# Other gather rates by stage in a one-core decoder layer, and half of one list's rows made by ACT

## The chip, the core and the metric

The kernel runs on one core of a Trainium2 chip. The metric is the device time of one execution in microseconds (us), as the median of several runs. The core has five instruction queues: PE (TensorE, matrix products), DVE (VectorE), ACT (ScalarE), POOL (GpSimd, which here issues all indirect DMAs) and SP (SyncE, which issues most other DMAs). Each queue runs its instructions in order and waits on semaphores of the others.

## What is computed

One decoder layer on 256 tokens of width 2048: attention, a PEER feed-forward, a gated embedding, with a layer norm behind each. The change lies in the PEER part, which the reference computes so:

```python
q = (xt @ wq).reshape(t, PEER_HEADS, PEER_QDIM)
sa = jnp.einsum('thc,nc->thn', qa, sub_keys[0]); sb = jnp.einsum('thc,nc->thn', qb, sub_keys[1])
va, ia = lax.top_k(sa, PEER_TOPK); vb, ib = lax.top_k(sb, PEER_TOPK)
cand = va[..., :, None] + vb[..., None, :]; cidx = ia[..., :, None] * PEER_NKEYS + ib[..., None, :]
top, sel = lax.top_k(cand, PEER_TOPK)
eidx = take_along_axis(cidx, sel); gates = softmax(top)
act = gelu(einsum('the d,td->the', u[eidx], x))
out = einsum('the,thed->td', gates * act, v[eidx])
```

Every token picks, in each of 8 heads, 16 of 16384 experts; an expert is one row of 2048 numbers in u and one in v.

## The kernel before

**Two ways for the experts.** The first 88 tokens go the sparse way: POOL gathers 128 rows of u at a time (one expert row for each of 128 partitions, 1 MB, tile `gb`, four buffers), DVE multiplies them with the tokens and sums (L951), later the same with rows of v (L961). That takes 88 gathers of u and 88 of v (`GROUPS`: 64 + 16 + 8). The other 168 tokens go the dense way: PE multiplies blocks of 128 experts with all 168 tokens, and gates are then set at the right places.

**The dense way has three stages.** *Direct blocks of u*: 68 blocks `ia`, straight from u (`u_block`, L1197; results in A0 and A1). *Listed blocks of u*: of the other 60 x 128 experts only those that some token picked, gathered by a list of their numbers: 40 blocks `b` (`CAPS[1]`), whose rows (`uf`, L1271) PE must first transpose (`ps_T`, L1280) before the products (L1289). *Blocks of v*: 46 and then 40 listed blocks (`CAPS`), each with a gather of v rows (`vf`) and one of weights (`wc`), L1256, both through POOL, up to LEAD = 4 blocks ahead; the products are L1341. DVE multiplies a block's `wc` with the u results in `weigh` (L1364).

**What has to happen beside it.** While PE computes the direct blocks, DVE selects the experts of the second tile of tokens (`topk_heads`), then ACT and DVE make one-hot flags of all picks which PE counts (`second_flags`: `eq` L884 or L837 and L838, `ohb` L887, counts L841), and from the counts comes the list of the second part (`list_work(flp, 1)`, the list made first), which ends in `idxV` and `idxW` (L1183, L1185). In its main loop each group of three columns needs `eqb`, two rows of `blk`, and `row`, a one-hot of the rank, all on DVE (L1165 to L1170). During the listed blocks of u the gates are built (`gate_work`: L1042, L1044 on DVE, L1048, L1049 on ACT, products `ps_G` L1056, L1057), the list of the first part is made, and the weights of the first part go out to HBM (`s_w`); during the first blocks of v the same happens to the gates of the second part. `gate_work` and the lists are Python generators, and `run(work, n)` puts n steps of them into the program after each block. `steps` says how many: 1 in the selection and the first tile's flags, 5 and 3 afterwards.

**How the gathers are paced.** `gathers(n)` after each block adds n to a sum, and each whole number in it puts one gather into the program, together with the DVE work on the gather three earlier (`run(sparse, 1)`, `use`). Up to the end of the direct blocks a gather is also preceded by a mark, a tiny DMA on SP's queue behind the weight loads, on which POOL waits (L980, L981). The rates are `GQ` in the query stage (13 times), 1.5 in direct blocks 0 to 4, then `GU`, in listed blocks `GUL`, in blocks of v `GVG` and `GV`. What is left is done at the last but three block of v (L1468); three blocks are held back for the end (`STAG`), their `weigh` comes after that, and the sums of the sparse tokens are taken between the banks of those three (`third_sums`).

Most of the instructions around the change keep their order as written (`keep`). The buffers of `uf` and `vf` are those of the weight loads (`sup`, tag `wf`, five buffers in turn).

Of the kernel before, what the change touches and what calls it, by code (L numbers as in the profile page):

```python
# [14 lines left out]
ALU = mybir.AluOpType  # L15
# [4 lines left out]
P = 128  # L20
# [36 lines left out]


GQ = 2.1
GU, GUL = 0.70, 1.35  # L60
GV, GVG = 0.55, 0.55
GSCALE = 2.0 ** 15
GB = 3

EARLY, HEARLY = 5, 2
# [95 lines left out]
def build(tc, a, out):  # L161
    nc = tc.nc
# [6 lines left out]
    def pbank(pool, name, tag="bank", bufs=4):  # L169
        return pool.tile([P, 512], F32, name=name, tag=tag, bufs=bufs)  # L170
# [385 lines left out]
    for c in range(NCH):  # L556
# [8 lines left out]
        for t in range(NT):  # L565
            nc.vector.scalar_tensor_tensor(x1[t][:, s], x1[t][:, s], ALPHA, pss[t],
                                           op0=ALU.mult, op1=ALU.add)
# [53 lines left out]
    io128 = gin.tile([P, P], F16, name="io128")  # L621
# [71 lines left out]
    keep = tc.keep_in_program_order  # L693
# [140 lines left out]
    def act_one_hot(dst, pool, neg):  # L834

        d = pool.tile([P, P], F16, name="dist", tag="dist", bufs=1)
        nc.scalar.activation(d, io128, AF.Abs, bias=neg)  # L837
        nc.scalar.activation(dst, d, AF.Relu, bias=1.0, scale=-1.0)  # L838
# [71 lines left out]
    def gathers(n):  # L910

        nonlocal due
        due += n
        while due >= 1:
            due -= 1
            run(sparse, 1)
# [183 lines left out]
    def list_work(oh, part):  # L1100

        nonlocal steps
        s0, ns = PARTS[part]
        m = m16[:, s0:s0 + ns]
        ps = pbank(pa, "ps_cols")
        keep(nc.tensor.matmul(ps[:ns, :P], m, ones16, start=True, stop=True))
        cols = oh.tile([P, P], F16, name="cols", tag="cols")
        keep(nc.vector.tensor_copy(cols[:ns], ps[:ns, :P]))
        yield
        ps = pbank(pa, "ps_used")  # L1110
        keep(nc.tensor.matmul(ps[:, ns:ns + 1], cols[:ns], ones16[:ns, :1], start=True, stop=True))
        keep(nc.tensor.matmul(ps[:, :ns], ahead, m, start=True, stop=False))
        keep(nc.tensor.matmul(ps[:, :ns], cols[:ns], ahead[:ns, :ns], start=False, stop=True))
        yield
        used = oh.tile([P, SEG1 + 1], F32, name="used", tag="used")
        keep(nc.vector.tensor_copy(used[:, :ns + 1], ps[:, :ns + 1]))
        pos = oh.tile([P, SEG1], F32, name="pos", tag="pos")[:, :ns]
        rank = oh.tile([P, SEG1], F32, name="rank", tag="rank")[:, :ns]
        u = used[:, :ns]

        keep(nc.vector.scalar_tensor_tensor(pos, lin[:, :ns], used[:, ns:ns + 1], u,
                                            op0=ALU.add, op1=ALU.subtract))
        keep(nc.vector.tensor_tensor(rank, u, pos, op=ALU.subtract))
        keep(nc.vector.tensor_tensor(rank, rank, m, op=ALU.mult))
        keep(nc.vector.tensor_tensor(pos, pos, rank, op=ALU.add))
        ov = gin.tile([P, 1], F32, name=f"ov{part}")
        keep(nc.vector.tensor_scalar(ov, used[:, ns:ns + 1], -float(CAPS[part] * P), 0.0,
                                     op0=ALU.add, op1=ALU.max))
        over.append(ov)
        if len(over) > 1:  # L1130
            keep(nc.vector.tensor_tensor(total, over[0], over[1], op=ALU.add))
        yield
        pi = oh.tile([P, SEG1], U32, name="pi", tag="pi")[:, :ns]
        pj = oh.tile([P, SEG1 + 1], U32, name="pj", tag="used")[:, :ns]
        pos16 = oh.tile([P, SEG1], F16, name="pos16", tag="pos16")[:, :ns]
        rank16 = oh.tile([P, SEG1], F16, name="rank16", tag="rank16")[:, :ns]
        keep(nc.vector.tensor_copy(pi, pos))
        keep(nc.vector.tensor_single_scalar(pj, pi, P - 1, op=ALU.bitwise_and))
        keep(nc.vector.tensor_single_scalar(pi, pi, 7, op=ALU.logical_shift_right))
        keep(nc.vector.tensor_copy(pos16, pi))  # L1140
        keep(nc.vector.tensor_copy(rank16, pj))
        if part:
            steps = 5
        yield

        ps = pbank(pa, "ps_list")
        made = []

        def products():
            ia0, n, row, blk = made.pop(0)  # L1150
            for j in range(n):
                keep(nc.tensor.matmul(
                    ps[:, :2 * SEG1].rearrange("p (i b) -> p i b", i=2)[:, :, :ns],
                    row[:, j], blk[:, :, j, :], start=ia0 + j == 0, stop=ia0 + j == ns - 1))

        for ia in range(0, ns, GB):
            n = min(GB, ns - ia)

            def cut(x):
                return x[:, ia:ia + n, None]  # L1160

            row = oh.tile([P, GB, P], F16, name="row", tag="ohb", bufs=OHB)
            blk = oh.tile([P, 2, GB, ns], F16, name="blk", tag="blk", bufs=3)
            eqb = oh.tile([P, GB, SEG1], F16, name="eqb", tag="eq", bufs=OHB)[:, :n, :ns]
            keep(nc.vector.tensor_tensor(eqb, io128[:, None, :ns].to_broadcast([P, n, ns]),  # L1165
                                         cut(pos16).to_broadcast([P, n, ns]), op=ALU.is_equal))
            keep(nc.vector.tensor_scalar(blk[:, 0, :n], eqb, lin[:, 0:1], None, op0=ALU.mult))
            keep(nc.vector.tensor_tensor(blk[:, 1, :n], eqb,
                                         cut(io128).to_broadcast([P, n, ns]), op=ALU.mult))
            keep(nc.vector.tensor_tensor(row[:, :n], io128[:, None, :].to_broadcast([P, n, P]),  # L1170
                                         cut(rank16).to_broadcast([P, n, P]), op=ALU.is_equal))
            made.append((ia, n, row, blk))
            yield
            if len(made) > 2:
                products()
        while made:
            products()
        ib = oh.tile([P, SEG1 + 1], F32, name="ib", tag="used")[:, :ns]
        iv = gin.tile([P, ns], U32, name=f"idxV{part}")
        iw = gin.tile([P, ns], U32, name=f"idxW{part}")  # L1180
        keep(nc.vector.tensor_copy(ib, ps[:, :ns]))
        pia = ps[:, SEG1:SEG1 + ns]
        keep(nc.vector.scalar_tensor_tensor(iw, ib, float(ns), pia, op0=ALU.mult, op1=ALU.add))  # L1183
        keep(nc.vector.tensor_scalar(ib, ib, float(s0 * NKEY), None, op0=ALU.add))
        keep(nc.vector.scalar_tensor_tensor(iv, pia, float(NKEY), ib, op0=ALU.mult, op1=ALU.add))  # L1185
        idxV[part] = iv
        idxW[part] = iw

    def run(work, n):

        for _ in range(n):
            if next(work, "end") == "end":
                return True
        return False
# [7 lines left out]
    def W_of(ia):  # L1202
        return A0[:, ia, :] if ia < SEG0 else A1[:, ia - SEG0, :]

    steps = 1
# [26 lines left out]
    for ia in range(SEG1):  # L1232
        if ia == EARLY:
            pools.close("earlyp")
            a1p = pools.open("a1p", "right", bufs=1)
            A1 = a1p.tile([P, SEG1 - SEG0, NDT], F32, name="A1")
        u_block(ia, W_of(ia))
        run(work, steps)
        gathers(GU if ia >= EARLY else 1.5)
    while not run(work, 1):  # L1240
        pass
    pools.close("flp", "tkl")
# [55 lines left out]
    work, listing = first_part(), first_list()  # L1298
# [15 lines left out]
    for b in range(CAPS[1]):  # L1314
        if b == CAPS[1] - 5:
            while not run(work, 1):
                pass
            while not run(listing, 1):
                pass
            pools.close("a1p", "a0p")  # L1320
            g2p = pools.open("g2p", "right", bufs=1)
            G2 = g2p.tile([P, SEG2, NDT], F32, name="G2")
            wcp = pools.open("wcp", "right", bufs=1)
        ps = pbank(pp, "ps_u")
        for c in range(4):
            turn(4 * b + c + 2)
            rows_mm(ps, turned.pop(0), c)
            if b < CAPS[1] - 5:
                run(work, 1)
        nc.scalar.activation(WL[:, b, :], ps[:, :NDT], AF.Gelu_apprx_tanh)  # L1330
        run(listing, 1)
        if b >= CAPS[1] - 4:
            fetch(wcp)
        gathers(GUL)
    pools.close("utp")
    work = gate_work(ohp, (G2,), *PARTS[1], 1, True)

# [50 lines left out]
    for b in range(CAPS[0]):  # L1388
        if b == CAPS[0] - LEAD:
            while not done:  # L1390
                done = run(work, 1)
            more = nc.values_load(total[0:1, 0:1], min_val=0, max_val=NIA * NKEY)
        v_blocks(1, wcp, half)
        gathers(GVG if b < 28 else GV)
    pools.close("ohp")
    wcq = pools.open("wcq", "left", bufs=1)
    for _ in range(LEAD + 1):
# [464 lines left out]
```

## Time and profile before

| | us |
|---|---|
| median of 3 runs | 1717.5 (1717.02 to 1719.36) |
| the profiled execution, its own time | 1715.06 |
| its span, first to last instruction | 1713.1 |
| direct blocks of u: first result to last | 537.4 to 864.5 |
| listed blocks of u: up to the first product of v's banks | to 1169.4 |
| blocks of v: held blocks begin | 1572.7 |

The times of stages are us from the span's start, read from the instructions in order of time (L1200 on ACT; L1348 and L1341 on PE). In the rows of the profile, a group shows the line, the engine, the operation, out<-in, the count, then busy us, mean ns of one, and the idle time of the engine just before with what ended it. A row in order of time begins with the start and the duration. A row of a window shows for each engine its busy us and instructions, then the clock that PE was granted (1.00 is full), the share of time that DMA was busy and GB/s.

### The profile page before, as it was taken

To read this page: it belongs to the slowest core of one execution; us is meant where nothing else is said; L and a number is where in the kernel's file an instruction comes from. 1 tells how busy PE (TensorE), PEld (TensorE's weight loads), DVE (VectorE), ACT (ScalarE), POOL (GpSimd) and SP (SyncE) were. 2 spreads that over 40 slices of the span, in tenths; PEclk is the share of its full clock that TensorE was granted. 3 is DMA by queue.
4 is the path that set the end of the run, shared out by engine and by line. 5 is a ranking of instruction groups with operands and counts; after the bars stand their busy time and mean duration, and the time that the engine had idled before them with its cause. 6 is when DMAs were issued, how large, how long until landed. Compare 5 with 4: busy or idle time off the path is not lost. (4 is left out here: it accounts for less than half of the span.)

```text
span 1713.1 us, 29137 instructions
## 1 busy us (share of the span) xinstructions
PE 1670.5 (98%) x11120; PEld 1550.0 (90%) x11120; DVE 1123.5 (66%) x2135; ACT 731.5 (43%) x1823; POOL 658.6 (38%) x615
## 2 busy tenths in 40 slices
PE   9999999999999999999959999989999999999998
PEld 7888888887889999999959999989999999999786
DVE  5565588763599679767877788837666223443676
ACT  5677468753111443347036677635553000000552
POOL 0143023203264422721174434528755666673000
PEclk9999999999999999999979999999999999999999
DMA  8645644584998999998779888899999999998571
GB/s 296 198 153 167 234 157 151 163 322 156 383 395 314 393 420 417 396 421 346 270 303 377 317 330 332 330 425 416 415 349 352 419 415 396 369 353 318 172 264 50
DMA packets 93996, 533.47 MB, mean 311 GB/s; under 512 B 12940, under 2 KB 16188, under 8 KB 41084
## 3 DMA queue, kind: packets, MB, share of 16 engines
q0 software_dynamic: 48912, 327.40, 48.6%
q1 hardware_dynamic: 43212, 201.02, 31.8%
q10 hardware_dynamic: 1728, 3.15, 0.5%
q8 instruction: 89, 1.46, 0.3%
q14 instruction: 55, 0.45, 0.1%
HBM read 515.70 MB, written 15.99 MB: 310 GB/s over the span
## 5 line engine op out<-in xcount | busy, mean ns | idle before, releaser
L1341 PE MATMUL ps_v<-wc,vf 128*128 128x168 f32 x2752 | 408.2, 308 | 1.9 <-DMA vf<-v_rows,idxV 1.6
L1341 PEld LDWEIGHTS ps_v<-wc,vf 128*128 128x128 f32 x2752 | 395.2, 191 | 3.2 <-issue 2.6
L212 PE MATMUL ps_u<-XF,wf 128*128 128x168 f32 x2016 | 303.5, 308 | 0.0
L212 PEld LDWEIGHTS ps_u<-XF,wf 128*128 128x128 f32 x2016 | 288.7, 190 | 2.0 <-issue 1.0
L122 DVE TENSOR_TENSOR wl<-wf,wh 128x1024 fp32r<-128x1024 f32 (+1 forms) x199 | 212.6, 1091 | 108.2 <-ACT wh L121 106.7
L121 ACT CAST wh<-wf 128x1024 fp32r<-128x1024 f32 (+1 forms) x199 | 172.1, 893 | 221.2 <-DMA wf<-ple_gate 109.0
L951 DVE SCALAR_TENSOR_TENSOR gb<-gb,xq 128x2048 f32<-128x2048 f32 x88 | 202.1, 2305 | 56.0 <-DMA gb<-u_rows,eig 55.9
L961 DVE SCALAR_TENSOR_TENSOR y<-gb,ew,y 128x2048 f32<-128x2048 f32 x78 | 182.9, 2345 | 77.5 <-DMA gb<-v_rows,eig 76.8
L1289 PE MATMUL ps_u<-XF,uT 128*128 128x168 f32 x1280 | 215.2, 311 | 0.1
L983 POOL DMA_INDIRECT gb<-u_rows,eig x88 | 100.6, 1143 | 231.4 <-DVE gb L951 117.7
L1289 PEld LDWEIGHTS ps_u<-XF,uT 128*128 128x128 f32 x1280 | 187.4, 192 | 0.9 <-ACT uT L1283 0.3
L200 PE MATMUL ps_qk<-X,wh 128*128 128x512 f32 x512 | 185.2, 401 | 0.0
L983 POOL DMA_INDIRECT gb<-v_rows,eig x88 | 118.5, 1347 | 126.0 <-DVE y L961 84.6
L1048 ACT ACTIVATE hi<-eq,ghf 128x68 f16<-128x68 f16 (+1 forms) x336 | 113.0, 336 | 84.6 <-DVE eq L1042 83.0
L202 PE MATMUL ps_qk<-X,wl 128*128 128x256 f32 x512 | 145.7, 285 | 0.0
L1256 POOL DMA_INDIRECT wc<-s_w,idxW x86 | 115.0, 1338 | 31.3 <-issue 25.8
L1256 POOL DMA_INDIRECT vf<-v_rows,idxV x86 | 93.0, 1081 | 87.3 <-PE ps_v L1341 38.3
L1283 ACT COPY uT<-ps_T 128x512 f32<-128x512 f32 x160 | 90.6, 581 | 73.6 <-PE ps_T L1280 67.9
L200 PEld LDWEIGHTS ps_qk<-X,wh 128*128 128x128 f32 x512 | 96.4, 188 | 21.9 <-issue 1.0
L212 PE MATMUL ps_q<-XF,wf 128*128 128x256 f32 x512 | 113.8, 379 | 0.5 <-ACT eb L581 0.5
L1049 ACT ACTIVATE lo<-eq,glf 128x68 f16<-128x68 f16 (+1 forms) x336 | 112.0, 333 | 0.0
L212 PEld LDWEIGHTS ps_q<-XF,wf 128*128 128x128 f32 x512 | 95.8, 190 | 13.1 <-ACT eb L581 0.9
(332 smaller groups left out, 2598.9 us busy)
## 6 DMA issues: line engine op xcount, KB each, us to landing
wf<-peer_u SPq DMA_DIRECT2D x63, 1024.0 KB
wf<-w_qk SPq DMA_DIRECT2D x64, 512.0 KB
wf<-w_out SPq DMA_DIRECT2D x32, 512.0 KB
wf<-peer_wq SPq DMA_DIRECT2D x16, 1024.0 KB
wf<-ple_gate SPq DMA_DIRECT2D x16, 1024.0 KB
wf<-w_v SPq DMA_DIRECT2D x16, 512.0 KB
wf<-w_sv SPq DMA_DIRECT2D x15, 512.0 KB
early<-peer_u SPq DMA_DIRECT2D x5, 1024.0 KB
```

The lines of the kernel that those rows point to most:

```text
L121: self.order(nc.scalar.copy(wh, src))
L122: self.order(nc.vector.tensor_tensor(wl, src, wh.bitcast(F32), op=ALU.subtract))
L200: nc.tensor.matmul(ps, wh[:, j * P:(j + 1) * P], xt[:, dt, :], start=dt == 0, stop=False)
L202: nc.tensor.matmul(ps[:, :T], wl[:, j * P:(j + 1) * P], xt[:, dt, :T], start=False, stop=dt == ND - 1)
L212: nc.tensor.matmul(ps[:, :T - t0], wf[:, dt * P:(dt + 1) * P], xt[:, dt, t0:], start=dt == 0, stop=dt == ND - 1)
L951: keep(nc.vector.scalar_tensor_tensor(g, g, 1.0, xq[i], op0=ALU.mult, op1=ALU.mult, accum_out=eact[i][:, j:j + 1]))
L961: keep(nc.vector.scalar_tensor_tensor(ys[i], g, ew[i][:, j:j + 1], ys[i], op0=ALU.mult, op1=ALU.add))
L983: keep(nc.gpsimd.indirect_dma_start(out=g, out_offset=None, in_=a[kind], in_offset=bass.IndirectOffsetOnAxis(ap=eig[i][:, 0, j:j + 1], axi ...
L1048: nc.scalar.mul(hi[:, j, :], eq[:, j, :], ghf[:, t])
L1256: keep(nc.gpsimd.indirect_dma_start(out=dst, out_offset=None, in_=src, in_offset=bass.IndirectOffsetOnAxis(ap=idx[:, b:b + 1], axis=0)))
L1289: nc.tensor.matmul(ps[:, :NDT], uT[:, j * P:(j + 1) * P], XF[:, d, NSP:], start=d == 0, stop=d == ND - 1)
L1341: return nc.tensor.matmul(psv[d // 3][:, d % 3 * NDT:(d % 3 + 1) * NDT], vf[:, d * P:(d + 1) * P], wc, start=False, stop=last and (d % 3 = ...
```

## The change

The rates are set anew. In direct blocks from 5 on, 0.50 as long as `steps` is 1 and 0.60 afterwards, where it was 0.70. In listed blocks of u 1.40 up to block 27 and 1.00 from there, where it was 1.35. In blocks of v 0.68, where it was 0.55. The list of the first part starts at listed block 3 in place of 0. In the list of the second part, every other group of `row` is made by ACT with `act_one_hot` (two ACT instructions for each of three columns), for which one more small DVE instruction makes the negative rank.

```diff
-GU, GUL = 0.70, 1.35
-GV, GVG = 0.55, 0.55
+GU, GUF, GUL, GULS = 0.50, 0.60, 1.40, 1.00
+GV = 0.68
...
         keep(nc.vector.tensor_copy(rank16, pj))
+        keep(nc.vector.tensor_scalar(rank, pj, -1.0, None, op0=ALU.mult))
...
-            keep(nc.vector.tensor_tensor(row[:, :n], io128[:, None, :].to_broadcast([P, n, P]),
-                                         cut(rank16).to_broadcast([P, n, P]), op=ALU.is_equal))
+            if part and ia % (2 * GB):
+                for j in range(n):
+                    act_one_hot(row[:, j, :], oh, rank[:, ia + j:ia + j + 1])
+            else:
+                keep(nc.vector.tensor_tensor(
+                    row[:, :n], io128[:, None, :].to_broadcast([P, n, P]),
+                    cut(rank16).to_broadcast([P, n, P]), op=ALU.is_equal))
...
-        gathers(GU if ia >= EARLY else 1.5)
+        gathers(1.5 if ia < EARLY else GU if steps == 1 else GUF)
...
         nc.scalar.activation(WL[:, b, :], ps[:, :NDT], AF.Gelu_apprx_tanh)
-        run(listing, 1)
+        if b > 2:
+            run(listing, 1)
...
-        gathers(GUL)
+        gathers(GUL if b < 28 else GULS)
...
         v_blocks(1, wcp, half)
-        gathers(GVG if b < 28 else GV)
+        gathers(GV)
```

`act_one_hot` (L834, unchanged) computes relu(1 - |column - rank|):

```python
nc.scalar.activation(d, io128, AF.Abs, bias=neg)
nc.scalar.activation(dst, d, AF.Relu, bias=1.0, scale=-1.0)
```

## The prediction

> **What bounds the kernel now.** I read the page first, then PE's waits, the busy time by stage, and last the instructions in order of time at each place where PE stops.
>
> ```profile
> span 1713.1 us, 29137 instructions
> PE 1670.5 (98%) x11120; PEld 1550.0 (90%) x11120; DVE 1123.5 (66%) x2135; ACT 731.5 (43%) x1823; POOL 658.6 (38%) x615
> PE   9999999999999999999959999989999999999998
> ```
>
> PE is the bound: 98% busy. Only what removes or adds idle PE time, or PE work at a lowered clock, changes the time. One slice in the middle (the 21st, 857 to 899 us) is at 5 tenths. The waits of PE name it:
>
> ```profile
> PE ps_G L1056 <- DVE ohb L1044: 14.1, 1, 14.1
> PE ps_T L1280 <- DMA uf<-u_rows,idxV: 5.0, 3, 2.5
> PE ps_cnt L841 <- DVE ohb L887: 1.7, 1, 1.7
> PE ps_v L1341 <- DMA vf<-v_rows,idxV: 1.6, 2, 1.1
> ```
>
> The 14.1 us lie where the direct blocks of u end and the listed blocks begin (all engines there, in order of time):
>
> ```profile
> 857.15 0.22 DVE L1185 SCALAR_TENSOR_TENSOR idxV<-ps_list,ib 128x60 uint32<-128x60 f32 x1
> 857.29 2.28 DVE L951 SCALAR_TENSOR_TENSOR gb<-gb,xq 128x2048 f32<-128x2048 f32 x1
> 864.46 0.31 ACT L1200 ACTIVATE A<-ps_u 128x168 f32<-128x168 f32 x1 [4.25 <-PE ps_u L212]
> 877.63 0.36 DVE L1042 TENSOR_TENSOR eq<-io,iaT 128x204 f16<-128x204 f16 x1
> 877.90 0.96 POOL L983 DMA_INDIRECT gb<-u_rows,eig  x1 [0.16 <-DVE gb L951]
> 878.54 0.24 PE L1056 MATMUL ps_G<-hi,ohb 128*128 128x68 f16 x1 [14.12 <-DVE ohb L1044]
> 879.16 0.94 POOL L1271 DMA_INDIRECT uf<-u_rows,idxV  x1 [0.30 <-PE ps_G L1056]
> ```
>
> The list (idxV) is complete at 857.3, the last direct block at 864.5. Yet from 857.3 to 877.6 DVE works off sparse dot products that are ahead of the first gate work in its queue, and POOL issues their gathers ahead of the first listed rows (uf), which start only at 879.2. Both queues are a backlog of token gathers:
>
> ```profile
> mark<-c_iota SPq DMA_DIRECT2D x78, 0.0 KB
> L983 POOL DMA_INDIRECT gb<-u_rows,eig x73 | 82.7, 1132 | 227.6 <-DVE gb L951 117.0 <-DVE TV L669 49.9 <-DVE eqb L1165 28.6
> ```
>
> One mark goes with each gather until the direct blocks end, so the program puts 78 gathers there (13 x 2.1 + 5 x 1.5 + 63 x 0.70 = 78.9); the second row, POOL's groups from 0 to 864.6 us, shows that 73 had been issued by then. What the stop costs, and the later stages:
>
> ```profile
> core 0: us, PE busy (x) PEld busy (x) DVE busy (x) ACT busy (x) POOL busy (x), PEclk, DMA share, GB/s
> 810.00:858.00 48.00, 48.00 (x366) 46.58 (x366) 39.46 (x109) 2.97 (x11) 5.51 (x10) 1.00 0.69 262
> 864.50:896.00 31.50, 13.88 (x85) 11.33 (x85) 26.02 (x47) 13.35 (x48) 27.29 (x19) 0.62 0.94 358
> 896.00:1100.00 204.00, 203.58 (x1778) 200.27 (x1777) 164.96 (x348) 142.53 (x444) 85.95 (x65) 1.00 0.86 334
> 1100.00:1170.00 70.00, 64.96 (x473) 63.40 (x473) 36.11 (x21) 24.40 (x49) 32.17 (x24) 0.98 1.01 420
> 1320.00:1440.00 120.00, 118.38 (x831) 117.92 (x830) 36.24 (x28) 0.59 (x1) 80.53 (x69) 1.00 1.02 414
> 1440.00:1560.00 120.00, 120.00 (x843) 119.42 (x841) 48.35 (x55) 3.84 (x7) 81.20 (x65) 1.00 0.97 366
> L1289 PE MATMUL ps_u<-XF,uT 128*128 128x168 f32 x25 | 5.4, 363 | 0.0
> L1280 PE MATMUL ps_T<-ident,uf 128*128 128x128 f32 x24 | 4.6, 349 | 0.0
> 1102.34 0.60 PE L1280 MATMUL ps_T<-ident,uf 128*128 128x128 f32 x4
> 1102.77 1.31 PE L1289 MATMUL ps_u<-XF,uT 128*128 128x168 f32 x8
> 1103.92 0.60 PE L1280 MATMUL ps_T<-ident,uf 128*128 128x128 f32 x4
> ```
>
> From 864.5 to 896 PE got through 24 transposes, 25 matmuls of ps_u (the two group rows, of that window) and 36 small ones. At the steady pace of the last three rows, four transposes take 0.43 us and eight matmuls 1.15, so this is 6 x 0.43 + 3.1 x 1.15, with 1.3 estimated for the small ones: 7.5 of 31.5 us. The stop costs 24.0 us, 17.6 of the window idle and the rest at a mean clock of 0.62.
>
> **The change, part by part.**
>
> **Fewer gathers beside the direct blocks.** In the code, the selection has 34 steps, the first tile's flags 6 more, the transposes 2: blocks 5 to 41 run with steps = 1 and take 0.50, the 26 after them 0.60. That is 34.8 + 18.5 + 15.6 = 68.9 gathers for 78.9, so 68 marks. As 73 were issued in time, the backlog at the boundary is gone; the 68th gather goes out with block 66. Before the flags, DVE has 50 dot products in its queue for 57 (53 and 60 gathers by block 41, the products three behind), and there it mostly waits for data. The next rows are a transfer of the page's last part, DVE's largest group from 715 to 750, ACT's conversion of the indices and DVE's first flag.
>
> ```profile
> uf<-u_rows,idxV POOLq DMA_INDIRECT x40, 10.4
> L951 DVE SCALAR_TENSOR_TENSOR gb<-gb,xq 128x2048 f32<-128x2048 f32 x8 | 18.3, 2297 | 17.5 <-DMA gb<-u_rows,eig 17.5
> 727.88 0.26 ACT L817 CAST ibT<-ps_gT 128x128 f16<-128x128 f32 x1
> 749.79 0.55 DVE L884 TENSOR_TENSOR eq<-io,iaT 128x384 f16<-128x384 f16 x1
> ```
>
> The flags need ibT (728.1) and begin at 749.8, behind those eight products (17.5 us of the 35 waiting for gathers); they can begin up to 21.7 us sooner, and the list with them. The uf buffers come free as PE ends blocks 63 to 67, at 4.56 us a block (4.25 + 0.31 in ACT's row above) from 846 on, so a list ready by then is early enough: the first listed rows land before the 864.5 at which PE needs them. I take 22 of the 24.0 us as gained. If the list came no earlier at all, uf would be issued at 857.5, land 10.4 us later and keep PE waiting for 3.4: a gain of some 20. Twice that loss with its slow clock makes the lower bound, 14; the upper is 24. What is late next is PE itself. PE's 1.7 us wait for a flag, and ACT's smaller ones beside it, shrink: -1.5 (0 to -2.5).
>
> **ACT makes rows of the list of the second part.** Of 20 groups, 10 lose one DVE comparison and gain 3 rows of two ACT instructions:
>
> ```profile
> L1170 DVE TENSOR_TENSOR row<-io,rank 128x384 f16<-128x384 f16 x20 | 11.0, 550 | 0.0
> L837 ACT ACTIVATE dist<-io,niaT 128x128 f16<-128x128 f16 x59 | 23.6, 401 | 1.8
> L838 ACT ACTIVATE eq<-dist 128x128 f16<-128x128 f16 x60 | 18.5, 309 | 3.1 <-PE ps_cnt L841 1.4
> ```
>
> DVE saves 10 x 0.55 = 5.5 us; ACT gains 30 x 0.71 = 21.3, in a stage where it is busy 2.97 of 48. The new rank instruction, a small one, falls once in each list: hidden on DVE, under 0.3 us if the list were late. I count nothing: the 22 us hold it.
>
> **The first part's list three blocks later.** It ends at block 30 in place of 27; its first reader is the fetch at block 36. Nothing, behind the blocks between; without that cover, a late fetch would stop PE at the start of v.
>
> **The listed blocks of u.** 28 x 1.40 + 12 x 1.00 = 51.2 for 54. Up to block 27 that is 0.05 x 2.3 = 0.1 us of DVE a block, hidden, as PE stood only 0.4 of 204 us there. In the last 12 blocks (the 1100 to 1170 row) the weights of the first part go out and DMA is saturated at 420 GB/s; PE waits 5.0 us for uf. There 4.8 gathers of 1.049 MB (128 rows of 8 KB) go: 12 us of DMA. Some of it is lag from before: -3.5 (0 to -6.4, the waits and the 0.98 clock).
>
> **The blocks of v.** 83 x 0.68 = 56.4 for 45.7. With the others that makes 176.5 for the 2 x 88 there are. At the pace of the last window (843 matmuls in 120 us, 32 a block: 4.56 us) 0.13 more a block is 30 GB/s: 366 becomes 396, and saturation is 414. Behind the 5.16 MB of the second part's weights (128 x 60 x 168 x 4 B), at about 1316, 414 - 366 = 48 GB/s were left to catch up, 108 us, which is the saturated window; now 18 are, which lasts to the end of v. When the vf waits (1.6 us) occurred, 40 us in, the arrears would be 1.2 MB larger: 2.9 us. I take +4, from 0 to the 28 that 11 moved gathers cost if none finds a gap (11 x 1.049 MB / 414 GB/s).
>
> **The last gather.** The 176th falls in the last block of the loop, behind the fetch of block 39:
>
> ```profile
> 1560.36 2.35 DVE L961 SCALAR_TENSOR_TENSOR gb<-gb,ew 128x2048 f32<-128x2048 f32 x1 [5.87 <-DMA gb<-v_rows,eig]
> 1563.57 0.93 POOL L1256 DMA_INDIRECT vf<-v_rows,idxV  x1 [2.37 <-PE ps_v L1341]
> 1566.46 0.33 DVE L1364 TENSOR_TENSOR wc<-wc,WL 128x168 f32<-128x168 f32 x1 [2.23 <-DMA wc<-s_w,idxW]
> 1572.71 5.37 PE L1341 MATMUL ps_v<-wc,vf 128*128 128x168 f32 x36 [0.30 <-PEq L1473]
> gb<-v_rows,eig POOLq DMA_INDIRECT x88, 9.9
> ```
>
> Before, the last product ended at 1562.7. Now its gather goes out at 1564.8 at the earliest and lands 9.9 later, 1574.7. Behind its product (2.35) in DVE's queue stand the weighings of the held blocks 38 and 39 (0.6), and PE's held matmuls wait for those: 1577.6 instead of 1572.7. With a dented clock I take +6 (0 to 8). The Trainium skill, "TensorE: Matmul & The Clock Gate", section on the HAM clock gate, has the clock halve after about 3.4 us of idling and recover after as much work: by it this stop alone would cost 4.9 + 1.7; the 0.62 above bears the halving out.
>
> **Sum**: -22 - 1.5 - 3.5 + 4 + 6 = -17.0. The profiled execution took 1715.06 us (span 1713.1 and 2.0 around it): 1698.1. The median, 1717.5, lies 2.4 above it: 1700.5.
>
> **Rivals.** *The costs in v do not show*: the last gather lands in time and DMA finds gaps, while the gains reach their bounds: -24 - 2.5 - 6.4 = -32.9, 1684.6. For it: PE waited only 1.6 us in 120 saturated ones. Against: the arithmetic of the last gather. *The boundary only half heals*: another DVE item, gate work or a late list, keeps PE from starting; the gain is 12 and no wait for flags goes: -12 - 3.5 + 4 + 6 = -5.5, 1712. For it: every engine's order is fixed beforehand, so one late item holds all behind it. *v gives it back, slower than before*: DMA carries no more than its mean there, the moved gathers cost the full 28: -22 - 1.5 - 3.5 + 28 + 6 = +7, 1724.5. It decides from 21 us of added waits in v on, that is, if at least 8 of 11 gathers find no gap. Against: 366 GB/s in the last 120 us beside 414 before them. The skill's "DMA: Bandwidth & Descriptors", Specifications, gives about 358 GB/s of HBM to a core, by which v would be bound like this; 414 for 120 us contradicts it. *Nothing happens*: the boundary waits for something else that the backlog hid, 1717.
>
> **How the numbers follow.** Forecast 0.60 (1690 to 1709 from its unknowns), no costs 0.13, half healed 0.15, given back 0.07, nothing 0.05. Range 1688 to 1713: it leaves out the given back case, nothing, and most of the no-cost one. About 0.2%, 3.4 us, is what a measurement here can tell. Slower by that much: given back and a little of the tail of nothing, 0.08; within it 0.05; faster 0.87.
>
> **What would show it.** 68 marks; idxV complete before about 846; uf issued as its buffer comes free, no wait of more than 2 us of ps_G or ps_T at the boundary, no clock below 1 there; the ps_T waits at the end of the listed blocks under 2 us; DMA near 414 GB/s through the second half of v with a few us of vf waits; DVE's last product about 5 us after PE could have begun the held blocks. The prediction is wrong if the boundary still stops PE for 10 us, or if the vf waits in v exceed 15.

## The result and the profile after

| | us | against the kernel before |
|---|---|---|
| before, median of 4 runs | 1717.26 (1716.89 to 1719.36) | |
| after, median of 4 runs | 1704.05 (1700.8 to 1705.25) | ratio 0.9918 [0.99, 0.9935] |
| after, the profiled execution | 1705.25 (span 1703.4) | 9.8 below 1715.06 |
| predicted, for the median | 1700.5 (1688 to 1713) | |

The kernel is faster by 13.2 us in the median, where 17.0 were forecast, so it ends 3.5 us above the forecast time. The span, which the stages below divide, is 9.7 shorter. From here on *U* is the direct blocks (to PE's last product of them), *UL* the listed blocks of u (to the last row of `WL`, the u results of a listed block), *V* the blocks of v up to the three held ones, *end* the rest; U ends with the end of that product, the other boundaries are starts in the rows of ACT and PE.

| | U ends | UL | V | end | span |
|---|---|---|---|---|---|
| before | 864.4 | 305.2 | 403.1 | 140.4 | 1713.1 |
| after | 864.4 | 280.6 | 404.1 | 154.4 | 1703.4 |
| difference | -0.1 | -24.6 | +0.9 | +14.0 | -9.7 |

On the page, PE's slices and the clock have lost the 5 in the middle; a lower slice stands near the end, where the clock is no longer full.

```profile
span 1703.4 us, 29145 instructions
...
PE 1667.9 (98%) x11120; PEld 1549.9 (91%) x11120; DVE 1120.4 (66%) x2127; ACT 754.0 (44%) x1883; POOL 678.5 (40%) x605
...
PE   9999999999999999999999999999999999997998
...
PEclk9999999999999999999999999999999999998999
```

PE's waits name the exchange: 14.1 us for `ohb` are gone, 10.5 us for a weighing (`wc`) have come.

```profile
PE ps_v L1348 <- DVE wc L1371: 10.5, 1, 10.5
PE ps_T L1286 <- DMA uf<-u_rows,idxV: 6.5, 4, 3.2
PE ps_v L1348 <- DMA vf<-v_rows,idxV: 2.7, 3, 1.2
...
PE ps_u L212 <- DMA wf<-peer_u: 1.2, 1, 1.2
```

**The boundary from U to UL**, in order of time, with the first flag, the list, the last gather, the first listed rows and what PE does:

```profile
725.93 0.56 DVE L884 TENSOR_TENSOR eq<-io,iaT 128x384 f16<-128x384 f16 x1 [2.65 <-ACT iaT L817]
...
835.42 0.22 DVE L1191 SCALAR_TENSOR_TENSOR idxV<-ps_list,ib 128x60 uint32<-128x60 f32 x1
...
854.79 3.03 POOL L983 DMA_INDIRECT gb<-u_rows,eig  x1 [4.07 <-DVE ew L942]
...
858.13 1.19 POOL L1277 DMA_INDIRECT uf<-u_rows,idxV  x1 [0.30 <-issue]
...
864.19 0.19 PE L1056 MATMUL ps_G<-hi,ohb 128*128 128x68 f16 x1
...
867.46 1.53 PE L1286 MATMUL ps_T<-ident,uf 128*128 128x128 f32 x12 [2.15 <-DMA uf<-u_rows,idxV]
```

The flags begin 23.9 us sooner (749.79 before), the list is done 21.7 us sooner (857.15 before). PE goes on at once with gate work and waits only 2.15 us for the first rows. Those are issued at 858.1, not at 846: the last sparse gather, which itself waited for DVE, is ahead of them in POOL's queue.

**The end.** The last gather is issued 1541.56; PE reaches the held blocks at 1549.0 and stands:

```profile
1541.56 0.94 POOL L983 DMA_INDIRECT gb<-v_rows,eig  x1 [0.30 <-issue]
...
1544.17 18.82 SPq L111 DMA_DIRECT2D wf<-ple_gate  x3
...
1557.40 2.35 DVE L961 SCALAR_TENSOR_TENSOR gb<-gb,ew 128x2048 f32<-128x2048 f32 x1 [7.44 <-DMA gb<-v_rows,eig]
1559.67 0.57 DVE L1371 TENSOR_TENSOR wc<-wc,WL 128x168 f32<-128x168 f32 x2
```

```profile
1549.00 0.52 PE L1348 MATMUL ps_v<-wc,vf 128*128 128x168 f32 x2 [0.30 <-PEq L1480]
1560.05 7.93 PE L1348 MATMUL ps_v<-wc,vf 128*128 128x168 f32 x34 [10.52 <-DVE wc L1371]
```

The gather takes 15.8 us to land; its product and two weighings follow, and PE's wait of 10.5 us ends with the first weighing. The 34 products that then remain take 7.93 us, where 36 took 5.37 before: the clock is low. The windows show the stages:

```profile
core 0: us, PE busy (x) PEld busy (x) DVE busy (x) ACT busy (x) POOL busy (x), PEclk, DMA share, GB/s
864.50:896.00 31.50, 29.30 (x250) 28.91 (x247) 16.93 (x37) 19.51 (x58) 14.32 (x12) 1.00 1.01 422
...
1300.00:1420.00 120.00, 117.30 (x822) 116.61 (x822) 40.12 (x28) 1.18 (x2) 88.84 (x69) 1.00 1.02 417
1420.00:1540.00 120.00, 120.00 (x842) 119.42 (x841) 56.22 (x61) 3.25 (x6) 95.58 (x72) 1.00 1.01 412
1540.00:1600.00 60.00, 47.56 (x276) 43.81 (x275) 26.50 (x49) 12.27 (x28) 4.70 (x8) 0.80 0.57 199
```

At the boundary PE is busy 29.30 of 31.5 us for 13.88. DMA now stays at 412 GB/s to the end of V, where it had eased to 366.

### The profile page after: what moved, and what is told of

Read it like the earlier page. It is cut to its first block, busy times and chain, and to the rows that moved or that the text cites. A ratio compares the mean times of both kernels' runs of the same rounds, so it can differ in the third digit from the quotient of the medians.

```text
span 1703.4 us, 29145 instructions
## 1 busy us (share of the span) xinstructions
PE 1667.9 (98%) x11120; PEld 1549.9 (91%) x11120; DVE 1120.4 (66%) x2127; ACT 754.0 (44%) x1883; POOL 678.5 (40%) x605
## 4 chain that ended last, share of the span: by engine, by line
PE 67%; DMA 13%; DVE 10%; issue 5%; POOL 4%; ACT 1%; POOLq 0%; SPq 0%; ACTq 0%; DVEq 0%
PE ps_v L1348 16%; PE ps_u L1295 9%; PE ps_qk L200 7%; PE ps_u L212 6%; DVE gb L951 4%; PE ps_qk L202 4%; PE ps_T L1286 4%; DMA uf<-u_rows,idxV 3%; PE ps_q L212 3%; DMA gb<-u_rows,eig 3%; DMA vf<-v_rows,idxV 3%; DMA gb<-v_rows,eig 2%; PE ps_v L219 2%; PE ps_v L220 2%; PE ps_v L221 2%
## 5 line engine op out<-in xcount | busy, mean ns | idle before, releaser
L1348 PE MATMUL ps_v<-wc,vf 128*128 128x168 f32 x2752 | 414.3, 310 | 13.5 <-DVE wc L1371 10.5
L983 POOL DMA_INDIRECT gb<-u_rows,eig x88 | 113.8, 1294 | 217.2 <-DVE gb L951 111.7
L983 POOL DMA_INDIRECT gb<-v_rows,eig x88 | 129.6, 1473 | 110.2 <-DVE y L961 44.6
L1262 POOL DMA_INDIRECT vf<-v_rows,idxV x86 | 107.0, 1244 | 63.1 <-PE ps_G L1057 30.5
L1262 POOL DMA_INDIRECT wc<-s_w,idxW x86 | 105.7, 1229 | 26.6 <-issue 24.4
```

The costliest lines, as they stand in the source:

```text
L983: keep(nc.gpsimd.indirect_dma_start(out=g, out_offset=None, in_=a[kind], in_offset=bass.IndirectOffsetOnAxis(ap=eig[i][:, 0, j:j + 1], axi ...
L1262: keep(nc.gpsimd.indirect_dma_start(out=dst, out_offset=None, in_=src, in_offset=bass.IndirectOffsetOnAxis(ap=idx[:, b:b + 1], axis=0)))
L1348: return nc.tensor.matmul(psv[d // 3][:, d % 3 * NDT:(d % 3 + 1) * NDT], vf[:, d * P:(d + 1) * P], wc, start=False, stop=last and (d % 3 = ...
```

## The experiments

The theory: three things make up the result. The rates beside the direct blocks heal the boundary; the ACT rows do nothing; and the last gather, put into the program within the last block of V, lands late and takes some 14 us back. The rivals are named in the expectations. Each ratio is to the kernel before, the stages as above (all from profiled executions, which lie up to 5 us from the median of their kernel).

| | median us | ratio [95%] | U ends | UL | V | end |
|---|---|---|---|---|---|---|
| e1_v_front | 1697.17 | 0.9884 [0.9858, 0.991] | 864.5 | 280.0 | 409.2 | 141.4 |
| e2_old_u_rates | 1720.45 | 1.002 [1.0006, 1.0033] | 864.2 | 301.8 | 411.0 | 140.4 |
| e3_dve_rows | 1705.93 | 0.9935 [0.992, 0.995] | 867.3 | 279.9 | 403.7 | 154.0 |
| e4_before_late_end | 1725.93 | 1.0047 [1.0029, 1.0064] | 863.9 | 304.0 | 409.1 | 148.1 |
| e5_weigh_first | 1704.48 | 0.9921 [0.9903, 0.9939] | 862.6 | 283.4 | 404.5 | 153.4 |
| e6_mix | 1693.12 | 0.9858 [0.9841, 0.9875] | 866.9 | 279.2 | 403.4 | 146.7 |
| e7_guls14 | 1697.92 | 0.9899 [0.9882, 0.9915] | 864.0 | 286.8 | 404.5 | 140.7 |
| e9_gv70 | 1698.05 | 0.9908 [0.9885, 0.9931] | 864.2 | 281.3 | 406.0 | 143.0 |

**e2_old_u_rates**: after, with the old rates in the direct blocks.

```diff
-GU, GUF, GUL, GULS = 0.50, 0.60, 1.40, 1.00
+GU, GUF, GUL, GULS = 0.70, 0.70, 1.40, 1.00
```

Expected: 

> The changed kernel with 0.70 a direct block throughout, everything else as changed (ACT rows, late first list, the new rates in u and v). Theory (the backlog of gathers made the stop at the boundary): the stop between direct and listed blocks returns, 15 to 24 us lost there; the gathers end 15 blocks earlier in v, so the end wait of about 13 us goes; together 1706 to 1714 us. Rival (the ACT rows, that is a list ready earlier, healed the boundary): no stop there, and with the end wait gone about 1690 us.

The whole gain goes: 1720.45, above the 1706 to 1714 expected. PE's longest waits, and the list and first rows in order of time:

```profile
PE ps_G L1056 <- DVE ohb L1044: 13.6, 2, 11.1
PE ps_T L1286 <- DMA uf<-u_rows,idxV: 5.1, 4, 2.2
PE ps_v L1348 <- DVE wc L1371: 4.1, 1, 4.1
```

```profile
853.83 0.22 DVE L1191 SCALAR_TENSOR_TENSOR idxV<-ps_list,ib 128x60 uint32<-128x60 f32 x1
...
875.29 0.24 PE L1056 MATMUL ps_G<-hi,ohb 128*128 128x68 f16 x1 [11.06 <-DVE ohb L1044]
875.91 0.94 POOL L1277 DMA_INDIRECT uf<-u_rows,idxV  x1 [0.30 <-PE ps_G L1056]
```

The list is complete before PE runs out of direct blocks, and PE stands all the same: the backlog of products and gathers is the cause, not the list. UL is 301.8, 21 us above after and 3.4 below before; from the first listed blocks on it is those 3 us ahead of before, as its list is (853.8 for 857.15). I put them down to the DVE time that the ACT rows save ahead of the backlog, which was not tried alone. V takes 411.0, 7 more than in after, which has the same rate there. Most of that is the last gather again, now in the middle of V (issued at 1498.39):

```profile
1510.84 2.35 DVE L961 SCALAR_TENSOR_TENSOR gb<-gb,ew 128x2048 f32<-128x2048 f32 x1 [2.83 <-DMA gb<-v_rows,eig]
...
1514.85 6.20 PE L1348 MATMUL ps_v<-wc,vf 128*128 128x168 f32 x32 [4.13 <-DVE wc L1371]
```

It lands after 12.4 us. A weighing waits behind its product in DVE's queue, and PE waits 4.1 us for that weighing. The 32 products that follow take 6.20 us, where 32 took 4.72 a block before. Together that is 5.6 us, which the expectation had left out.

**e3_dve_rows**: after, with no rows on ACT.

```diff
-            if part and ia % (2 * GB):
+            if False:
```

Expected: 

> The changed kernel with all rows of the list of the second part made by DVE again, everything else as changed. Theory (the list was ready some 20 us before POOL sent for its first rows, so its length is off the path): idxV complete about 5 us later, at 840, the boundary and the time unchanged, 1704 us within 3. Rival (the list bounds the boundary): the stop grows by about 5 us, 1709.

1705.93 against 1704.05, with ratios that overlap: the rows on ACT make no difference that can be measured. In its trace `idxV` comes at 841.2 and not 835.4, so the edit does what it says, 5.8 us, but ahead of a reader (POOL, which sends for the first listed rows at 859.7 here and at 858.1 in after) that is late for another reason. U ends 2.9 us later there; in e6, which has the ACT rows, it ends 2.5 us later, so I don't put that down to the rows.

**e4_before_late_end**: the kernel before, with its rate in V lowered just so far that the last gather falls in the last block of the loop, as in after.

```diff
-GV, GVG = 0.55, 0.55
+GV, GVG = 0.523, 0.523
```

Expected: 

> The kernel before with 0.523 in place of 0.55 a block of v, so that its 176th gather falls in the last block of the loop as in the changed kernel; v is then less loaded than before. Theory A (place alone, landing in about 10 us as reckoned in the prediction): PE waits 5 to 6 us at the held blocks, time 1723 to 1726 us. Theory B (whatever the load, the last gather shares DMA with the gate weights and lands in 15 us or so): a wait of about 10 us and a slow clock behind it, 1729 to 1733 us. Rival (place does not matter, only the load of v): no wait, 1717 us.

The gather falls where it should, and the end grows by 7.7 us:

```profile
1569.85 0.94 POOL L983 DMA_INDIRECT gb<-v_rows,eig  x1 [0.30 <-issue]
1572.21 12.96 SPq L111 DMA_DIRECT2D wf<-ple_gate  x3
...
1577.04 0.52 PE L1341 MATMUL ps_v<-wc,vf 128*128 128x168 f32 x2 [0.30 <-PEq L1473]
1579.57 2.35 DVE L961 SCALAR_TENSOR_TENSOR gb<-gb,ew 128x2048 f32<-128x2048 f32 x1 [4.72 <-DMA gb<-v_rows,eig]
1582.22 7.91 PE L1341 MATMUL ps_v<-wc,vf 128*128 128x168 f32 x34 [4.65 <-DVE wc L1364]
```

It is issued 7.2 us before PE reaches the held blocks, as in after (7.4), and the gate weights go out some 2.5 us behind it in both. But it lands in 9.7 us, not 15.8. In this V the place of the gather costs 7.7 us, then; what makes the other 6 of after's 14 is taken up behind the experiments. V grew by 6 us too, half of it in waits for the gate work's `G` (3.3 us), which I had not foreseen and did not follow up.

**e1_v_front**: after, with more gathers in the first 28 blocks of V and fewer later, so that the last one comes some two blocks sooner.

```diff
-GV = 0.68
+GVG, GV = 0.85, 0.62
```

Expected: 

> The changed kernel with the gathers of v put earlier: 0.85 a block in the first 28 blocks of v and 0.62 after, so that the 176th gather falls three blocks earlier. Theory (the end waits because the last gather is placed in the last block of the loop): the 10.5 us wait of ps_v for wc and the slow clock behind it go, the last stage (held blocks to end) falls from 154 to about 141 us, time about 1691 us. Rival (v is bound by DMA, and the wait is only where the arrears show): the waits of PE for vf grow by as much as the end gains, time 1701 to 1706.

The median, 1697.17, lies between the two expectations. The stop at the end is gone (141.4, 13 less than after), and 5 us are paid in V, in waits for rows of v (at 1333) and for the gate work's `G`:

```profile
PE ps_v L1348 <- DMA vf<-v_rows,idxV: 3.5, 1, 3.5
PE ps_G L1056 <- DVE G L1067: 2.5, 2, 1.8
```

The last gather (1538.0) landed in 9.8 us, before the held blocks at 1553.7.

**e5_weigh_first**: after, with the weighings of the held blocks queued on DVE ahead of the last products.

```diff
         if b == N1 - STAG - 1:
+            fetched[:] = [weigh(block) for block in fetched]
```

Expected: 

> The changed kernel with the weighing of the three held blocks put into DVE's queue ahead of the last sparse products. Theory (the held blocks' matmuls wait only for DVE's order): PE goes on at once with the held blocks and waits next at the sums of the sparse tokens, 5.8 us of work later, for the last product: the wait of 10.5 us becomes one of about 4.6, time 6 to 8 us less than the changed kernel, about 1697 us. Rival (the held blocks' own rows or weights land that late): the same wait, for DMA, and 1704 us.

No gain: 1704.48, where the theory had 1697. The wait for `wc` is gone, and two others stand in its place, for rows of v and for DVE's sums of the held banks (`XF`), which are still behind the last product:

```profile
1554.59 6.47 PE L1348 MATMUL ps_v<-wc,vf 128*128 128x168 f32 x32 [3.32 <-DMA vf<-v_rows,idxV]
1559.51 2.35 DVE L961 SCALAR_TENSOR_TENSOR gb<-gb,ew 128x2048 f32<-128x2048 f32 x1 [7.34 <-DMA gb<-v_rows,eig]
...
1564.91 0.44 PE L1421 MATMUL ps_y<-ident,XF 128*128 128x128 f32 x2 [3.84 <-DVE XF L1363]
```

So moving the weighings forward is not enough, as the landings are late: 16.2 us for the last gather (from 1543.32), and the rows of a held block, issued at 1542.08, hold PE until 1554.59.

**e9_gv70**: after, with 0.70 in all of V.

```diff
-GV = 0.68
+GV = 0.70
```

Expected: 

> The changed kernel with 0.70 in place of 0.68 a block of v: the 176th gather three blocks earlier, the load of v up by 2 hundredths of a gather a block. Theory (only the place of the last gather makes the end wait): the last stage falls from 154 to about 141 us and v stays near 404 us, 1691 us. Rival (arrears of DMA in v): v itself grows by several us, as where the gathers were moved to its first blocks (409), and the time is about 1697.

Expected were 1691 or 1697. The 0.02 shorten the end from 154.4 to 143.0 and add 2 to V. The last gather goes out 15.8 us ahead of the held blocks (1535.66) in place of 7.4, and lands in 11.2. The median is 1698.05, but the interval of its ratio overlaps with that of after: the stage is told apart by the traces, the whole kernel is not.

**e7_guls14**: after, with 1.40 kept to the end of UL, and 0.64 in V.

```diff
-GU, GUF, GUL, GULS = 0.50, 0.60, 1.40, 1.00
-GV = 0.68
+GU, GUF, GUL, GULS = 0.50, 0.60, 1.40, 1.40
+GV = 0.64
```

Expected: 

> The changed kernel with 1.40 gathers in the last twelve listed blocks too (4.8 more there) and 0.64 a block of v; the 176th falls three blocks earlier. Theory A of the listed blocks (the number of gathers there sets PE's waits for uf, as the prediction had it): these waits grow from 4.3 us by several, the stage from 280 to 285 or more. Theory B (the weights going out in one burst set them, whatever the gathers): waits and stage as they were. Of the end: the wait is gone, and v, with less to carry, takes no longer than 404: by B 1690 us, by A 1695 or more.

1697.92, again with an interval that overlaps with that of after: the end is as short as before (140.7), and UL is 6.2 longer than after. PE's waits between 1100 and 1170 in it, and then in after:

```profile
PE ps_T L1286 <- DMA uf<-u_rows,idxV: 6.5, 2, 4.7
```

```profile
PE ps_T L1286 <- DMA uf<-u_rows,idxV: 3.9, 2, 3.2
```

Measured from block 30 of UL on (1084.0 here, 1082.0 in after, to 1150.8 and 1144.9), the tail takes 66.8 us, 3.9 more than in after. In the five traces with 1.00 there (after, e1, e3, e5, e9) it takes 60.8 to 63.0, so the 4.8 gathers cost between 3.8 and 6.0 us: 0.8 to 1.3 each, not the 2.5 that a megabyte takes at 420 GB/s. The waits, the stage and the time are nearer to theory A.

**e6_mix**: after, with 1.10 in the tail of UL, 0.76 in the first 28 blocks of V and 0.65 in the others.

```diff
-GU, GUF, GUL, GULS = 0.50, 0.60, 1.40, 1.00
-GV = 0.68
+GU, GUF, GUL, GULS = 0.50, 0.60, 1.40, 1.10
+GVG, GV = 0.76, 0.65
```

Expected: 

> The changed kernel with 1.10 in the last twelve listed blocks, 0.76 in the first 28 blocks of v and 0.65 after: 176th gather three blocks earlier, v loaded between the other two. Theory (place of the last gather and the arrears of v are separate costs): no wait at the held blocks, v between 403 and 408 us, about 1693 us. Rival (the order that the scheduler finds, not the load, makes v's length): v as long as in the others within 2 us, with no order by load.

The best of all: 1693.12 (1688.89 to 1698.0), 11 us below after, with intervals that don't touch. The profiled execution is the slowest of its four (1698.0). In it UL and V are as short as in after, and the end is longer than before by 6.3 where after's is by 14.0; the last gather had landed by 1541.5. DVE's and PE's rows show what is late next:

```profile
1554.09 2.50 DVE L122 TENSOR_TENSOR wl<-wf,wh 128x512 fp32r<-128x512 f32 x4 [8.42 <-ACT wh L121]
1556.50 1.26 DVE L1363 SCALAR_TENSOR_TENSOR XF<-XF,ps_v 128x504 f32<-128x504 f32 x2
...
1557.23 0.44 PE L1421 MATMUL ps_y<-ident,XF 128*128 128x128 f32 x2 [2.34 <-DVE XF L1363]
```

The conversion of the next weights (`wl`) is ahead of the sums (`XF`) in DVE's queue and waits for ACT's part of it (`wh`).

## Why the prediction was right, point by point

- **The boundary**: right, in mechanism and in size. Predicted -22 of 24.0. ACT's `WL` rows of blocks 12 to 30 come between 21.4 and 25.2 us sooner, 23.4 in the mean (block 30: 1105.7 before, 1082.0 after), with U's end unchanged. The chain held link by link: 68 marks, flags and list 24 and 22 us sooner, clock 1.00. One link did not: the first rows were issued at 858.1, not when a buffer came free, since POOL's queue still held sparse gathers; it cost PE 2.15 us, just over the 2 us that the prediction named as a sign. e2 shows that the rates are the cause.
- **PE's wait for a flag**, -1.5: the wait is gone (e2 has it back, 0.8 and smaller ones), but U ends at 864.4 in both. A new wait of 1.2 us for the weights of the direct blocks stands in its place. Worth nothing.
- **The ACT rows, the deferred list, the rank**, 0: right for the rows (e3). The deferred list and the rank were not tried alone.
- **The tail of UL**, -3.5: too much. The stage's -24.6 leaves 1.2 behind the boundary's 23.4, and the waits for `uf` in the tail went from 5.0 to 4.3. The sign named was under 2. Part of it is the count: the 4.8 gathers are the distance from 1.40 to 1.00, while from the 1.35 of before it is 12 x 0.35 = 4.2, or 10.5 us of DMA in place of 12. And fewer still left the tail: from the `WL` row of block 27 to the last one POOL issued 17 before and 15 after. That each one has a price there is borne out by e7 (0.8 to 1.3 us). What else holds the waits up is open. Less time for DMA, now that PE no longer stops at the boundary, is not the answer that the runs give: DMA eases to a share of 0.83 between 940 and 1080 in after, and e2, which has that stop and the lower rate in the tail, still waits 5.1 us for `uf`.
- **The arrears in V**, +4: V is 0.9 longer, with 2.7 us of waits for `vf` in place of 1.6. That DMA would be full to the end of V was right (412 GB/s). That this costs time is not shown: V takes 403.7 and 404.5 in e3 and e5 at the same rate, and 409.1 in e4 at a lower one. That rows of v are read up to four blocks ahead may have hidden the price; this was not tried.
- **The last gather**, +6 (0 to 8): the step that failed in size, +14.0 and outside its bounds. The queueing was as written (gather in the last block, product, weighings, held products; issued 7.4 us before the held blocks, where 7.9 was worked out). The term took 9.9 us for the landing, the median of all 88 in a V with spare DMA. Here it took 15.8. e4 tells the parts apart: with a landing of 9.7 the place alone costs 7.7, clock included. The fuller V alone doesn't make the rest, 6.1 us of landing: in after the 88 land in 10.1 in the median, and in e9, whose V carries more, the last one takes 11.2. The DMA queues show what moved between the issue of the last gather and its product (packets, MB, share of 16 engines; q0 is POOL's, q1 SP's). First after with its median, then e9, then e4:

```profile
q0 software_dynamic: 581, 3.89, 59.8%
q1 hardware_dynamic: 286, 2.09, 31.6%
gb<-v_rows,eig POOLq DMA_INDIRECT x88, 10.1
```

```profile
q0 software_dynamic: 708, 4.61, 100.7%
```

```profile
q0 software_dynamic: 405, 2.62, 70.8%
q1 hardware_dynamic: 147, 1.11, 33.6%
```

The term that the prediction left out is the 2.09 MB of gate weights on SP's queue. At 412 GB/s they are an estimated 5.1 us, without which the landing would be about 10.7. How much of them gets in ahead hangs on how full POOL's queue still is: e4 has them at the same place, but with 1.3 MB less of POOL's the gather had landed when 1.11 MB of theirs had moved. This is read from bytes; a kernel with those weights alone moved later was not tried.
- **The clock in this stop**: the wait of 10.5 us and e4's of 4.65 were followed by the same slow products, 7.93 and 7.91 us for 34, where 36 took 5.37: 2.6 us or more. The Trainium skill, "TensorE: Matmul & The Clock Gate", section on the HAM clock gate, has the clock recover after about 3.4 us of work, by which the prediction's estimate was 1.7; the runs give more, and the same for both lengths of the wait.
- **The sum**: -23.4 - 0.1 - 1.2 + 0.9 + 14.0 = -9.8, the span's -9.7 but for rounding, for -17.0 forecast. The last gather is 8.0 above its term; the others are off by -1.4, +1.4, +2.3 and -3.1, which nearly cancel. That is luck. The median fell by 13.2 and so lies nearer to the forecast than the sum does, which is luck too: the profiled execution was the slowest of after's four, and that of before lay under its median.
- **The rivals**: *half healed* gave -5.5, and the span's -9.7 lies between that and the forecast, but the boundary healed fully. *v gives it back* is wrong by its own price, 28 us in V for the 0.9 measured; what came back came from one gather.

## What to carry to other kernels

Work moved out of a crowded stage goes into the queues of another one, and the last item of it has the dearest place: find where the last transfer is issued, how long one takes to land at the load that you make, what other queues start to move beside it, and what it holds behind it in each queue. Here other rates for the same gathers, so that the last one was two blocks sooner, were worth 11 us more (e6). That number is for e6 as a whole, which also has other rates in UL and V; the profiled executions put 7.7 us of it into the end.

## What was not expected of the hardware

- DMA at 412 to 417 GB/s for 240 us on end costs PE little (2.7 us of waits) as long as nothing has to be in time. Single gathers of 1 MB hardly land later for it (10.1 us in the median for 9.9). The last one took 9.2 us in before, 9.0 to 11.2 in e6, e1, e7 and e9, 12.4 in e2, and 15.8 to 16.4 only in after, e3 and e5, where 2.1 MB of another queue moved beside POOL's 3.9 to 4.1. The Trainium skill's "HBM Reference", Specifications (TRN2), has a core streaming alone at about 425 GB/s, and the 417 agree, better than the per-core share that the prediction cites.
- PE's clock falls to half while PE is busy. In e7, where no wait precedes them, the small products of the sums (128 x 32) begin at 1561; in the rows of five-microsecond windows the clock is full up to 1565 and half afterwards, with PE busy throughout. In e6, behind a wait of 2.34 us, they begin at 1557.5, and the mean of 0.82 up to 1560 with 0.50 after it puts the drop at an estimated 1558.2: 0.7 us after the first of them, for some 4 in e7. First e7, then e6 (PE's busy time and count alone, then clock, DMA share and GB/s):

```profile
1555.00:1560.00 5.00, 4.70 (x34) 1.00 0.86 291
1560.00:1565.00 5.00, 4.93 (x44) 1.00 0.95 294
1565.00:1570.00 5.00, 5.00 (x26) 0.50 0.05 21
```

```profile
1555.00:1560.00 5.00, 2.77 (x18) 0.82 0.66 208
1560.00:1565.00 5.00, 5.00 (x26) 0.50 0.15 62
```

With about 14 more pairs of the small products at 0.43 us in place of 0.22, in e6, that makes 2.9 us beside the 2.34: most of the 6.0 by which e6's end is longer than e7's.
